# Requesting the keys' factors one pair of heads ahead, every other pair's into borrowed buffers

## The chip, the cores and the metric

One core of a Trainium2 chip runs one program. The metric is the device time of one launch in microseconds (us), as the median of several runs; the profile is of one further execution. TensorE (PE in the rows) multiplies, VectorE (DVE) and ScalarE (ACT) work elementwise, GpSimd (POOL) here only issues transfers, and so does SyncE (SP). PEld is TensorE's weight load.

## The reference

One layer of a diffusion backbone over 256 latent tokens with 256 context tokens, model width 2048: modulation from `c`, a combined input projection, attention with 8 heads beside a gated MLP over chunks, a merge with sigmoid gates, an output projection and a SwiGLU feed-forward part. What bears on the change is attention, with keys normalized by head:

```python
k = _rms(jnp.concatenate([k_nope, k_rope], axis=-1), qk_norm_k)
...
s = jnp.einsum('bqhd,bkhd->bhqk', qi, k, preferred_element_type=jnp.float32) * scale
p = jax.nn.softmax(s, axis=-1)
o = jnp.einsum('bhqk,bkhd->bqhd', p.astype(v.dtype), v, preferred_element_type=jnp.float32)
```

## The kernel before

Activations lie in the on-chip memory with channels on the 128 partitions. Weights stream through ten buffers `raw` of 128x1024 (512 KB), requested by SyncE in the program's order. Each half is split into a rounded part `whi` (ScalarE, L230) and the rest `wlo` (VectorE, L231), and the products run in both parts (`mm3`, `mm_wides`; every matmul is recorded at L244).

The layer runs in stages: modulation and input projections, the chunk MLP, queries and keys, attention, merge and output projection, feed-forward. Attention alone would leave TensorE idle while a softmax runs, so `fill(n, rate)` puts independent work between its parts: `n` halves of gate products, and for each of them `rate` steps of the second modulation (`background`; ATT_RATE is 2.9). Such a step takes one `raw` tile as it landed and adds it, scaled, into `acc` on VectorE (L416). At the end of a block of 16 tiles the sums go through DRAM: four small stores `m_d` (L439), then a load of `sh` (L442), on POOL's queue. VectorE adds a bias to `sh` at L397. These blocks are what stands on POOL's queue beside the requests of the change.

The keys are not normalized by themselves. One factor per key and head, the reciprocal root of the mean square, is computed for all heads in `rk` (to L754), stored to DRAM as `rk_d` by four stores (L757), and multiplied into the scores later. The attention loop (L776) takes the heads in four pairs. At the start of a pair two transfers (L782) request the factors of its two heads, each a row of 512 numbers repeated on 128 partitions (256 KB), into a slot of the pool `g`, which holds 60 slots of 128x512. For each of two halves `qt` of the queries the pair's scores go to two banks (L786, L790). Then for each head VectorE multiplies the scores by the factors and takes the maximum of a row (L794), makes the bias `nb` (L798), ScalarE takes the exponential with its sum `sm` (L800), VectorE inverts the sum and divides (L801, L802), and TensorE transposes the probabilities (L805) with the identity matrix in `cst`. ScalarE copies them out (L807), `fill` follows (L809), and after both halves the products with the values (L814).

`rst` (128x512) holds the reciprocal roots of the first norm; its last reader is the first modulation (L371), before the input projections end. `cst` holds constants: the identity and a permutation, then from column 2P on 512 columns of cosines and sines for the rotary step (`rcos`, `rsin`, read last at L472 and L473 for the queries), then small selection matrices. A scheduler of the framework sets the order in which each engine's queue holds its instructions, by its own estimate of when operands are ready, places slots, and adds a wait where two instructions touch the same bytes. Each engine works through its queue in that order and waits at the first instruction whose operands are missing.

Of the kernel before, what the change touches and what calls it, by code (L numbers as in the profile page):

```python
# [13 lines left out]
P = 128  # L14
# [4 lines left out]
TOK = SEQ + CTX  # L19
GRID_W = 64  # L20
HEADS = 8
# [91 lines left out]
def block_kernel(  # L113
# [25 lines left out]
    nc = tc.nc  # L139
# [13 lines left out]
    def uid():  # L153
        cnt[0] += 1
        return cnt[0]

    def slot(dt=F32):
        return gp.tile([P, 512], dt, tag="g", name=f"g{uid()}")

    def small(cols, name, bufs=8):  # L160
        return sp.tile([P, cols], F32, tag=name, name=f"{name}{uid()}", bufs=bufs)

    def mmbank():
        return pm.tile([P, 512], F32, tag="mm", name=f"mm{uid()}")

    def auxbank():
        return pa.tile([P, 512], F32, tag="aux", name=f"ax{uid()}")
# [4 lines left out]
    cst = cp.tile([P, CST_END], F32, name="cst")  # L172
# [70 lines left out]
    def mm(out, lhsT, rhs, start=True, stop=True):  # L243
        nc.tensor.matmul(out, lhsT, rhs, start=start, stop=stop)  # L244
# [33 lines left out]
    def split_to(dst_hi, dst_lo, src):  # L278
        S.activation(dst_hi, src, AF.Copy)  # L279
        V.tensor_tensor(out=dst_lo, in0=src, in1=dst_hi.bitcast(F32), op=ALU.subtract)  # L280
# [22 lines left out]
    rst = cp.tile([P, TOK], F32, name="rst")  # L303
# [150 lines left out]
    def background(rate):  # L454
        bg_state[0] += rate
        while bg_state[0] >= 1.0:
            bg_state[0] -= 1.0
            if next(bg, 1) is None:
                bg_state[1] += 1
# [166 lines left out]
    def fill(n, rate):  # L626
        for _ in range(n):
            if next(gi, 1) is None:
                background(rate)
# [59 lines left out]
    for c in range(3):  # L689
        w = W(flat(wuq, c * P * WCOLS, WCOLS), WCOLS)  # L690
        for i in range(2):
# [12 lines left out]
            else:  # L704
                S.activation(d, ps, AF.Copy, scale=pcol(PR_GQ + 1))
                r = slot()
# [48 lines left out]
    rk_d = dp.tile([HEADS, TOK], F32, name="rk_d")  # L755
    for i in range(4):
        nc.gpsimd.dma_start(rk_d[2 * i:2 * i + 2, :], rk[32 * i:32 * i + 2, :])  # L757

    fill(UQ_GATES[4], GATE_RATE)
    vals = []  # L760
    w = W(flat(wuv, 0, WCOLS), WCOLS)
# [13 lines left out]
    ao = []  # L775
    for p in range(HEADS // 2):  # L776
        pair = (2 * p, 2 * p + 1)
        rkb, pts = {}, {}
        for h in pair:
            rkb[h] = slot()  # L780
            r = 2 * (h % 4) + h // 4
            nc.gpsimd.dma_start(rkb[h], rk_d[r:r + 1, :].to_broadcast([P, 512]))  # L782
        for qt in range(2):
            ps = [auxbank(), auxbank()]
            for e, h in enumerate(pair):
                mm(ps[e], qnope[p][:, e * 256 + qt * P:e * 256 + (qt + 1) * P], kn[h], True, False)  # L786

            for e in range(2):
                rows64 = slice(e * ROPE, (e + 1) * ROPE)
                mm(ps[e], qrot[p][rows64, qt * P:(qt + 1) * P], krot[rows64, :], False, True)  # L790
            for e, h in enumerate(pair):
                t = slot()
                mx = small(1, "mx")
                V.tensor_tensor_reduce(out=t, in0=ps[e], in1=rkb[h], scale=1.0, scalar=-3.0e38,  # L794
                                       op0=ALU.mult, op1=ALU.max, accum_out=mx)
                col = qt * 8 + e * 4 + p
                nb = small(1, "nb")
                V.tensor_tensor(out=nb, in0=mx, in1=nrq[:, col:col + 1], op=ALU.mult)  # L798
                sm = small(1, "sm")
                exp = S.activation(t, t, AF.Exp, bias=nb, scale=rq[:, col:col + 1], accum_out=sm)  # L800
                V.reciprocal(sm, sm)  # L801
                V.tensor_scalar_mul(t, t, sm)  # L802
                tp = auxbank()
                for k in range(4):
                    nc.tensor.transpose(tp[:, k * P:(k + 1) * P], t[:, k * P:(k + 1) * P], ident)  # L805
                pt = slot()
                S.activation(pt, tp, AF.Copy)  # L807
                pts[h, qt] = pt
            fill(ATT_GATES[2 * p + qt], ATT_RATE)  # L809
        for h in pair:  # L810
            ops = auxbank()
            for qt in range(2):
                for k in range(4):
                    mm(ops[:, qt * P:(qt + 1) * P], vals[k * 2 + h // 4][:, (h % 4) * P:(h % 4 + 1) * P],  # L814
                       pts[h, qt][:, k * P:(k + 1) * P], k == 0, k == 3)
            t = slot(F32R)
            split_to(t[:, 0:256], t[:, 256:512], ops[:, 0:256])
            ao.append(t)
# [128 lines left out]
    for f in range(FT):  # L947
# [10 lines left out]
        pair = [mmbank(), mmbank()]  # L958
# [177 lines left out]
```

## Time and profile before

| | us |
|---|---|
| median of 3 runs (lowest to highest) | 1457.03 (1454.49 to 1457.60) |
| the profiled execution's own time | 1455.91 |
| its span, first to last instruction | 1454.1 |
| TensorE busy in it | 1422.4 (98%) |
| VectorE busy | 1018.6 (70%) |
| ScalarE busy | 772.6 (53%) |

Where the rows speak of idle time, the arrow names what ended it, inferred from the semaphores. The granted clock is TensorE's, as a share of 2.4 GHz. A landing is counted from the issue of a request to its last byte.

### The profile page before, as it was taken

The numbers are of one execution on the slowest core, as the hardware profiler recorded it, in microseconds if no ns is written. First come the engines' busy times: TensorE is split into PE (matmuls) and PEld (weight loads), VectorE is DVE, ScalarE is ACT, GpSimd is POOL, SyncE is SP. The second block draws the span as 40 slices with busy tenths as digits, with TensorE's granted clock in tenths as the row PEclk, the third lists the DMA queues.
The fourth block names the chain that finished last, engine by engine and source line by source line (L and its number), as shares of the span: only waits on it lengthen the run. The fifth ranks groups of instructions, "written<-read, shape, count | busy, mean of one in ns | idle before, by whom it ended". The sixth has DMA issues, their size and how long they took to land.

```text
span 1454.1 us, 23911 instructions
## 1 busy us (share of the span) xinstructions
PE 1422.4 (98%) x8782; PEld 1215.1 (84%) x8782; DVE 1018.6 (70%) x1738; ACT 772.6 (53%) x1432; POOL 22.2 (2%) x44
## 2 busy tenths in 40 slices
PE   6999999999989999999999999999999999999998
PEld 4898899886767799988788888888888888888887
DVE  2676579896688688999866666666666667786553
ACT  4655457555534554555566555555555554444442
POOL 0000000000101000000000000000000000000000
PEclk9999999999999999999999999999999999999999
DMA  9987874785499498999553555555555568898560
GB/s 366 350 318 266 316 297 140 253 287 190 144 313 314 175 362 329 324 353 391 175 183 135 192 188 186 192 188 189 187 190 189 188 202 308 309 361 302 198 213 33
DMA packets 104167, 356.08 MB, mean 245 GB/s; under 512 B 12520, under 2 KB 14824, under 8 KB 104048
## 3 DMA queue, kind: packets, MB, share of 16 engines
q1 hardware_dynamic: 102096, 350.82, 67.0%
q0 software_dynamic: 1952, 3.72, 1.0%
q8 instruction: 69, 1.13, 0.3%
q14 instruction: 50, 0.41, 0.1%
HBM read 352.36 MB, written 2.13 MB: 244 GB/s over the span
## 4 chain that ended last, share of the span: by engine, by line
PE 65%; DVE 4%; DMA 1%; issue 1%; ACT 0%; DVEq 0%; ACTq 0%
PE mm L244 62%; PE ax L244 2%; DVE acc L416 1%; DMA raw<-in_wmod_dram 1%; DVE wlo L231 1%; PE ax L805 0%; DVE g L802 0%; ACT g L800 0%; DVE g L405 0%; DVE g L890 0%; DVE g L794 0%; DVE g L870 0%; DVE g L892 0%; ACT whi L230 0%; DVE g L402 0%
## 5 line engine op out<-in xcount | busy, mean ns | idle before, releaser
L244 PE MATMUL mm<-g,whi 128*128 128x512 f32 (+1 forms) x3456 | 878.6, 347 | 0.8 <-ACT g L702 0.5
L230 ACT ACTIVATE whi<-raw 128x512 fp32r<-128x512 f32 x897 | 557.3, 630 | 500.9 <-PE mm L244 349.9
L231 DVE TENSOR_TENSOR wlo<-raw,whi 128x512 fp32r<-128x512 f32 x897 | 604.1, 687 | 259.1 <-ACT whi L230 253.4
L244 PE MATMUL mm<-g,wlo 128*128 128x256 f32 x2656 | 588.7, 282 | 0.6 <-DVE wlo L231 0.6
L244 PEld LDWEIGHTS mm<-g,wlo 128*128 128x128 f32 x2656 | 495.3, 190 | 79.5 <-DVE wlo L231 1.3
L244 PEld LDWEIGHTS mm<-g,whi 128*128 128x128 f32 x3456 | 540.0, 191 | 22.1 <-issue 11.0
L244 PE MATMUL mm<-whi,g 128*128 128x512 f32 x992 | 308.3, 391 | 0.0
L244 PEld LDWEIGHTS mm<-whi,g 128*128 128x128 f32 x992 | 186.2, 188 | 41.3 <-issue 2.5
L244 PE MATMUL mm<-wlo,g 128*128 128x512 f32 x496 | 193.2, 390 | 0.2 <-DVE wlo L231 0.2
L416 DVE SCALAR_TENSOR_TENSOR acc<-raw,silw,acc 128x1024 f32<-128x1024 f32 x120 | 153.4, 1278 | 17.7 <-DMA raw<-in_wmod_dram 17.1
L244 PEld LDWEIGHTS mm<-wlo,g 128*128 128x128 f32 x496 | 93.1, 188 | 21.2 <-issue 1.1
L554 DVE TENSOR_TENSOR g<-mm,g 128x512 f32<-128x512 f32 x60 | 41.1, 686 | 26.4 <-PE mm L244 25.9
L279 ACT ACTIVATE g<-g 128x256 fp32r<-128x256 f32 (+1 forms) x106 | 41.9, 414 | 13.7 <-DVE g L973 8.2
L280 DVE TENSOR_TENSOR g<-g,g 128x256 fp32r<-128x256 f32 (+1 forms) x106 | 43.2, 424 | 7.4 <-ACT g L279 7.3
L971 DVE TENSOR_TENSOR g<-mm,g 128x256 f32<-128x256 f32 x88 | 33.3, 419 | 17.3 <-ACT g L970 17.2
L970 ACT ACTIVATE g<-mm 128x256 f32<-128x256 f32 x88 | 29.0, 381 | 30.9 <-PE mm L244 30.9
L244 PE MATMUL ax<-g,g 128*128 128x128 f32 (+2 forms) x224 | 42.6, 374 | 0.0
L244 PE MATMUL ax<-raw,silw 128*32 128x256 f32 (+1 forms) x576 | 33.4, 359 | 3.7 <-DMA raw<-in_wmod_dram 3.7
L244 PEld LDWEIGHTS ax<-g,g 128*128 128x128 f32 (+1 forms) x224 | 26.6, 190 | 11.5 <-issue 9.6
L244 PEld LDWEIGHTS ax<-raw,silw 128*32 128x32 f32 x576 | 16.9, 109 | 16.0 <-DMA raw<-in_wmod_dram 5.8
L800 ACT ACTIVATE g<-g,nb,rq 128x512 f32<-128x512 f32 x16 | 13.0, 812 | 17.5 <-DVE nb L798 17.4
L375 ACT ACTIVATE g<-g,m 128x256 f32<-128x256 f32 x32 | 17.6, 592 | 8.3 <-DVE m L364 5.3
(140 smaller groups left out, 471.1 us busy)
## 6 DMA issues: line engine op xcount, KB each, us to landing
raw<-in_wmod_dram SPq DMA_DIRECT2D x192, 512.0 KB, 6.3
raw<-in_wffi_dram SPq DMA_DIRECT2D x176, 512.0 KB, 3.2
raw<-in_wffo_dram SPq DMA_DIRECT2D x88, 512.0 KB, 4.9
raw<-in_wgate_dram SPq DMA_DIRECT2D x56, 512.0 KB, 4.7
raw<-in_win_dram SPq DMA_DIRECT2D x48, 512.0 KB, 7.7
raw<-in_wout_dram SPq DMA_DIRECT2D x32, 512.0 KB, 7.5
raw<-in_wbrs_dram SPq DMA_DIRECT2D x16, 512.0 KB, 9.2
raw<-in_wbra_dram SPq DMA_DIRECT2D x16, 512.0 KB, 6.5
```

The source lines that it names most:

```text
L230: S.activation(hi[:, :e], raw[:, q:q + e], AF.Copy)
L231: V.tensor_tensor(out=lo[:, :e], in0=raw[:, q:q + e], in1=hi[:, :e].bitcast(F32), op=ALU.subtract)
L244: nc.tensor.matmul(out, lhsT, rhs, start=start, stop=stop)
L279: S.activation(dst_hi, src, AF.Copy)
L280: V.tensor_tensor(out=dst_lo, in0=src, in1=dst_hi.bitcast(F32), op=ALU.subtract)
L375: S.activation(v, v, AF.Identity, bias=m[:, 2 * jj + s:2 * jj + s + 1], scale=m[:, 2 * n + 2 * jj + s:2 * n + 1 + 2 * jj + s])
L416: V.scalar_tensor_tensor(out=acc, in0=w.raw[0], scalar=sil[:, k, 0:1], in1=acc, op0=ALU.mult, op1=ALU.add)
L554: V.tensor_tensor(out=acc[i], in0=ps, in1=acc[i], op=ALU.add)
L800: exp = S.activation(t, t, AF.Exp, bias=nb, scale=rq[:, col:col + 1], accum_out=sm)
L970: S.activation(d, ps[:, 256:512], AF.Copy)
L971: V.tensor_tensor(out=d, in0=ps[:, 0:256], in1=d, op=ALU.add)
```

## The change

The two requests move out of the loop into `key_rows(p)`. It is called for pair 0 right after the stores of `rk_d`, ahead of the gate products and the values, and for pair p + 1 at the start of pair p. Pairs 0 and 2 take slots of `g` as before; pairs 1 and 3 take `rst` and the 512 columns of cosines and sines in `cst`.

```diff
@@ -756,6 +756,17 @@
     for i in range(4):
         nc.gpsimd.dma_start(rk_d[2 * i:2 * i + 2, :], rk[32 * i:32 * i + 2, :])
 
+    rkb = {}
+
+    def key_rows(p):
+
+
+        for h in (2 * p, 2 * p + 1):
+            rkb[h] = slot() if p % 2 == 0 else (rst, cst[:, 2 * P:2 * P + TOK])[h % 2]
+            r = 2 * (h % 4) + h // 4
+            nc.gpsimd.dma_start(rkb[h], rk_d[r:r + 1, :].to_broadcast([P, 512]))
+
+    key_rows(0)
     fill(UQ_GATES[4], GATE_RATE)
...
@@ -775,11 +786,9 @@
     ao = []
     for p in range(HEADS // 2):
         pair = (2 * p, 2 * p + 1)
-        rkb, pts = {}, {}
-        for h in pair:
-            rkb[h] = slot()
-            r = 2 * (h % 4) + h // 4
-            nc.gpsimd.dma_start(rkb[h], rk_d[r:r + 1, :].to_broadcast([P, 512]))
+        pts = {}
+        if p + 1 < HEADS // 2:
+            key_rows(p + 1)
         for qt in range(2):
```

The diff also moves the scheduler's order. Lines from L757 on stand 9 to 11 lines later in the new file (L782 is now L767, L794 is L803, L802 is L811, L805 is L814).

POOL's queue from the stores of `rk_d` on, with what each request waits for (DMASW and DMAHW: a landing of POOL's or SyncE's transfers; the rest: an instruction of that engine). Before:

```order
L757 DMA rk_d<-g_4439 2x512 [waits DVE_49]
L782 DMA g_4546<-rk_d 128x512 [waits DMASW2_49,DMASW1_49,DMASW3_49,DMASW0_49,PE_49]
L782 DMA g_4548<-rk_d 128x512 [waits PE_49]
L442 DMA sh_158<-m_d_4823 128x8x1 [waits DMASW6_49,DMASW7_49,DMASW1_49,DMASW0_49]
L782 DMA g_4922<-rk_d 128x512 [waits DMAHW2_49,PE_49]
L782 DMA g_4924<-rk_d 128x512 [waits DMASW4_49,PE_49]
L439 DMA m_d_5268<-g_5266 16x1x16 [waits DMASW5_49,Activation_49]
L782 DMA g_5298<-rk_d 128x512 [waits DMAHW1_49,PE_49]
L782 DMA g_5300<-rk_d 128x512 [waits DMASW2_49,DVE_49,PE_49]
L782 DMA g_5659<-rk_d 128x512 [waits DMASW4_49,DVE_49,PE_49]
```

Now:

```order
L757 DMA rk_d<-g_4439 2x512 [waits DVE_49]
L767 DMA g_4454<-rk_d 128x512 [waits DMAHW2_49,DMASW0_49,PE_49]
L767 DMA g_4456<-rk_d 128x512 [waits DMASW1_49,PE_49]
L767 DMA rst<-rk_d 128x512 [waits DMASW2_49]
L767 DMA cst<-rk_d 128x512 [waits DMASW3_49]
L442 DMA sh_158<-m_d_4825 128x8x1 [waits DMASW3_49,DMASW2_49,DMASW4_49,DMASW1_49,DMASW0_49]
L767 DMA g_4924<-rk_d 128x512 [waits DMASW5_49,PE_49]
L767 DMA g_4926<-rk_d 128x512 [waits DMASW6_49,PE_49]
L767 DMA rst<-rk_d 128x512 [waits DMASW7_49,DVE_49]
L767 DMA cst<-rk_d 128x512 [waits DVE_49]
L439 DMA m_d_5270<-g_5268 16x1x16 [waits Activation_49]
```

Pair 1's two requests stand behind pair 0's, ahead of the first block's load of `sh`; pair 2's have its old place; pair 3's stand right behind, with a wait for VectorE.

TensorE's queue at the first transposes of pair 0 (`ax`), among the gate products (`whi` and `wlo` are the halves of a weight tile). Before:

```order
L244 MATMUL mm_4589<-g_1570,wlo_4655 128x256
L244 MATMUL mm_4590<-g_1574,wlo_4655 128x256
L244 MATMUL mm_4590<-g_1855,whi_4658 128x512
L244 MATMUL mm_4589<-g_1855,wlo_4659 128x256
L805 MATMUL ax_4565<-cst,g_4556 128x128 x4
L244 MATMUL mm_4590<-g_1855,wlo_4659 128x256
```

Now:

```order
L244 MATMUL mm_4591<-g_1273,whi_4609 128x512
L244 MATMUL mm_4592<-g_1273,whi_4609 128x512
L244 MATMUL mm_4591<-g_1273,wlo_4610 128x256
L244 MATMUL mm_4592<-g_1273,wlo_4610 128x256
L814 MATMUL ax_4567<-cst,g_4558 128x128 x4
L244 MATMUL mm_4591<-g_1277,whi_4609 128x512
L244 MATMUL mm_4592<-g_1277,whi_4609 128x512
```

The transposes have moved 15 matmuls ahead: they stood in the products of operand `g_1855`, and stand behind those of `g_1273`. On VectorE the first factor step of the pair has moved ahead of three weight splits that stood before it.

VectorE's queue at the first factor step of pair 1 (the ISA row; `rst` is the borrowed buffer). Before:

```order
L231 TENSOR_TENSOR wlo_5041<-raw_5038,whi_5040 128x512
L231 TENSOR_TENSOR wlo_5045<-raw_5038,whi_5044 128x512
L794 ISA g_4932,mx_4933<-ax_4926,g_4922 128x512
L416 SCALAR_TENSOR_TENSOR acc_4829<-raw_5084,silw,acc_4829 128x1024
L397 TENSOR_TENSOR sh_158<-sh_158,prm 128x8
L416 SCALAR_TENSOR_TENSOR acc_4829<-raw_5088,silw,acc_4829 128x1024
L801 RECIPROCAL sm_4937<-sm_4937 128x1
L231 TENSOR_TENSOR wlo_5138<-raw_5135,whi_5137 128x512
L802 TENSOR_SCALAR g_4932<-g_4932,sm_4937 128x512
```

Now:

```order
L231 TENSOR_TENSOR wlo_5043<-raw_5040,whi_5042 128x512
L803 ISA g_4934,mx_4935<-ax_4928,rst 128x512
L231 TENSOR_TENSOR wlo_5047<-raw_5040,whi_5046 128x512
L416 SCALAR_TENSOR_TENSOR acc_4831<-raw_5086,silw,acc_4831 128x1024
L810 RECIPROCAL sm_4939<-sm_4939 128x1
L397 TENSOR_TENSOR sh_158<-sh_158,prm 128x8
L416 SCALAR_TENSOR_TENSOR acc_4831<-raw_5090,silw,acc_4831 128x1024
L811 TENSOR_SCALAR g_4934<-g_4934,sm_4939 128x512
```

The factor step has moved ahead of one weight split. Between it and the division stand one split, two accumulations and the bias of `sh`, as before, in another order.

## Rows read from the trace of the kernel before

**Rows 1.** Busy us by stage: PE, PEld, DVE, ACT, POOL (instructions), clock, DMA share, GB/s
```profile
360.00:512.00 152.00, 142.15 (x780) 108.31 (x779) 112.93 (x202) 78.48 (x155) 15.04 (x27) 0.98 0.69 235
480.00:512.00 32.00, 30.10 (x184) 22.61 (x183) 17.75 (x40) 20.20 (x43) 2.27 (x5) 1.00 0.42 152
512.00:690.00 178.00, 178.00 (x1166) 161.96 (x1166) 165.19 (x242) 92.23 (x167) 6.92 (x14) 1.00 0.95 354
720.00:1440.00 720.00, 720.00 (x3813) 616.69 (x3812) 461.80 (x758) 386.12 (x706) 0.00 (x0) 1.00 0.60 210
```

**Rows 2.** TensorE's waits, 366 to 512 us: total, times, longest
```profile
PE ax L805 <- DVE g L802: 9.6, 10, 3.7
```

**Rows 3.** POOL's timeline: start, us, engine, line, operation, tiles, idle time before
```profile
366.83 2.22 POOL L757 DMA_DIRECT2D rk_d<-g  x4 [366.39 <-DVE g L294]
371.42 1.12 POOL L782 DMA_DIRECT2D g<-rk_d  x2 [2.37 <-PE mm L244]
...
404.53 1.09 POOL L782 DMA_DIRECT2D g<-rk_d  x2
...
446.76 1.09 POOL L782 DMA_DIRECT2D g<-rk_d  x2
```

**Rows 4.** Issues at 366.8, 371.4, 372.0, 404.5 and 446.8: KB, us to landing
```profile
rk_d<-g POOLq DMA_DIRECT2D x1, 4.0 KB, 3.5
...
g<-rk_d POOLq DMA_DIRECT2D x1, 256.0 KB, 3.5
...
g<-rk_d POOLq DMA_DIRECT2D x1, 256.0 KB, 4.3
...
g<-rk_d POOLq DMA_DIRECT2D x1, 256.0 KB, 7.9
...
g<-rk_d POOLq DMA_DIRECT2D x1, 256.0 KB, 6.5
```

**Rows 5.** VectorE's timeline in pairs 1 and 2
```profile
412.52 0.69 DVE L794 CUSTOM_DVE_ANT_0 g<-ax,g 128x512 f32<-128x512 f32 x1 [3.29 <-DMA g<-rk_d]
...
416.34 0.48 DVE L802 TENSOR_SCALAR g<-g,sm 128x512 f32<-128x512 f32 x1
...
422.53 0.48 DVE L802 TENSOR_SCALAR g<-g,sm 128x512 f32<-128x512 f32 x1
...
453.44 0.69 DVE L794 CUSTOM_DVE_ANT_0 g<-ax,g 128x512 f32<-128x512 f32 x1 [2.37 <-PE mm L244]
...
457.78 0.48 DVE L802 TENSOR_SCALAR g<-g,sm 128x512 f32<-128x512 f32 x1
```

**Rows 6.** TensorE's timeline in pairs 1 and 2
```profile
402.18 6.51 PE L244 MATMUL ax<-g,g 128*128 128x128 f32 x40
...
416.97 1.09 PE L805 MATMUL ax<-cst,g 128*128 128x128 f32 x4 [3.66 <-DVE g L802]
...
424.93 0.60 PE L805 MATMUL ax<-cst,g 128*128 128x128 f32 x4
...
458.41 0.63 PE L805 MATMUL ax<-cst,g 128*128 128x128 f32 x4 [2.49 <-DVE g L802]
```

**Rows 7.** Busy time in stretches of 2 us behind the two gaps
```profile
420.00:422.00 2.00, 2.00 (x7) 1.71 (x7) 1.50 (x4) 1.23 (x3) 0.00 (x0) 0.50 0.82 244
422.00:424.00 2.00, 2.00 (x12) 1.71 (x12) 2.00 (x3) 0.64 (x1) 0.00 (x0) 0.85 0.96 375
...
458.00:460.00 2.00, 1.59 (x11) 1.53 (x12) 2.00 (x4) 0.60 (x1) 0.00 (x0) 1.00 0.97 320
```

**Rows 8.** TensorE's and VectorE's timeline in pair 0
```profile
377.19 0.63 PE L244 MATMUL mm<-g,whi 128*128 128x512 f32 x2
...
380.23 0.63 PE L805 MATMUL ax<-cst,g 128*128 128x128 f32 x4 [0.21 <-DVE g L802]
...
381.20 0.69 DVE L794 CUSTOM_DVE_ANT_0 g<-ax,g 128x512 f32<-128x512 f32 x1
...
384.14 0.49 DVE L802 TENSOR_SCALAR g<-g,sm 128x512 f32<-128x512 f32 x1
```

## The prediction

> **What bounds the kernel now.** I read the table by stage first, then the waits of the attention stage, then the queues around them. The stage table shows TensorE busy for all of 512 to 690 us and of 720 to 1440 us, and for 142.15 of 152.00 us between 360 and 512, the stretch that holds attention [rows 1]. So what attention loses stays lost to the end, and what it gets back is got back, unless a later transfer takes it (a rival below). TensorE's waits between 366 and 512 us are of one kind: ten times, for 9.6 us together, the transposes of the probabilities wait for VectorE's last step, the division L802 [rows 2].
>
> Two of the ten make up 6.2 us, and both begin at the first score-times-factor step of a pair (L794). POOL's timeline shows when the keys' factors are requested: pair 1's at 404.53, pair 2's at 446.76 us, each at the start of its pair [rows 3]. The landings are 7.9 and 6.5 us after the request [rows 4], at 412.4 and 453.3. VectorE's timeline has L794 at 412.52 after 3.29 us of idleness, and at 453.44 after 2.37 [rows 5]: about 0.1 us behind the landing, both times. The second idle time is put down to TensorE; by those times it is the factors too. On TensorE each becomes a gap ahead of the transposes: 3.66 us up to 416.97 and 2.49 us up to 458.41 [rows 6]. After the longer gap the granted clock reads 0.50 (1.2 GHz); 422 to 424 has 0.85, so full speed is back at 422.6. After the shorter it stayed at 1.00 [rows 7]. Pair 3's factors are not waited for. Pair 0's come in just as VectorE turns to them: requested at 371.42 [rows 3], landed after 3.5 us [rows 4].
>
> **Pair 1.** Its factors are now requested at about 372 us and go into the two borrowed buffers, whose own readers are long done: nothing on POOL waits for them but the landing of two writes. So L794 waits for the scores alone. They are finished when the 40 matmuls of 402.18 are, at 408.69 [rows 6]. VectorE, one weight split further along, was free at 409.23 (412.52 less 3.29), so with L794 ahead of that split it is free at 408.6. I put L794 at 408.7. From L794 to the end of L802 it was 4.30 us (412.52 to 416.82 [rows 5]); the same kinds of steps stand between them in the new order. L802 then ends at 413.0, and TensorE comes to the transposes at 413.31 (416.97 less 3.66). The gap of 3.66 goes whole: **-3.7 us**, at least the 3.3 of VectorE's idleness.
>
> **The clock.** Without the gap no fall: from 416.97 to 422.6 TensorE worked at half speed, so 2.8 us are lost there. Not all of it comes back, because VectorE is next: the second head's transposes stood at 424.93 [rows 6], 7.96 us after the first, so at full speed 5.2 us after them, at 418.5. VectorE's part of that head starts 3.8 us sooner, not 6.5: L802 ran 422.53 to 423.01 there [rows 5], so 419.2 now, and the transposes follow at 419.4. I leave 0.9 us: **-1.9 us**, between -1.0 (the 0.9 twice) and -2.8.
>
> **Pair 2.** Its slots are read out by pair 0's products, so POOL requests it where pair 1's request stood, some 40 us before it is needed. L794 moves up by its idleness, L802 (ended 458.26 [rows 5]) to 455.9, and TensorE is there at 455.92 (458.41 less 2.49 [rows 6]). **-2.3 us**, between -2.1 (0.2 from L802 to the transposes) and -2.5, the whole gap.
>
> **Pair 3.** Its two requests wait on POOL for pair 1's last L794. Behind them stands the mod2 block's own store, which comes later by the program. Nothing gained, nothing lost: 0.
>
> **Pair 0.** Here the change costs something. The requests now wait for one write of the factors each, no longer for all four; the first write landed 3.5 us [rows 4] after 366.83, at 370.3, which lets the request out 0.5 us sooner, near 370.9. With 3.5 us to land and 0.1 to start, L794 comes at 374.5 instead of 375.05. But the order of TensorE's queue now has the first transposes 15 matmuls sooner: they stood at 380.23, after 0.21 us of waiting, and are now due at 377.19 [rows 8]. The second head's chain from L794 to the end of L802 took 3.43 us (381.20 to 384.63 [rows 8]); so L802 ends at 377.9, the transposes start at 378.1, and TensorE waits 0.9 where it waited 0.2: **+0.7 us**, between 0 and, if the row lands no sooner than before, +1.2. The weight splits set back behind L794 are for tiles that TensorE comes to only after the transposes' old place, over 3 us on: no cost. No instruction is added or dropped; there are eight requests before and after.
>
> Sum against the profiled execution of 1455.91 us: -3.7 -1.9 -2.3 +0.7 = -7.2, **1448.7 us**. That execution lies 1.1 us below the median shown; from the median the same gain would give 1449.8.
>
> What a request takes to land decides all this: the rows have 3.5 us in a quiet stretch, 7.9 and 6.5 in busy ones [rows 4], and my sum goes by them. The Trainium skill, "DMA: Bandwidth & Descriptors", section "Anatomy of one DMA", gives a fixed part of about 2.0 us and the bytes at 436 GB/s, by my estimate 2.6 us for 256 KB. By that, pair 1's factors would have been there at 407.1, ahead of the scores, and asking sooner would gain nothing there. The trace shows three times as long, and the measurement decides; what the rule would make of the time is the last rival.
>
> **Rivals.**
> *Pair 0 pays.* If the first row lands only when its second did (372.0 and 4.3, so 376.3 [rows 4]), since four now queue up, L794 is at 376.4, L802 ends at 379.9, and TensorE waits 2.8 us instead of 0.2. That lies between the gap that kept the clock (2.49) and the one that lost it (3.66): 1450.6, or with another 2.8 us of clock 1453.4. For it: four requests instead of two. Against: the first one issued is the first to be served in every pair of the rows.
>
> *VectorE keeps the time.* It is busy for 112.93 of the stage's 152 us [rows 1], and most of its steps take what a transfer brings; what is freed may be met at once by the next weight's landing. Then only VectorE's idleness in one pair is gained, 3.3 us: 1452.6. Against: in pair 1 the weights for the next accumulations were there by the time the factors were, since VectorE ran from L794 to L802 in 4.30 us of nearly unbroken work [rows 5].
>
> *Slower.* TensorE enters 512 to 690 some 7 us sooner, where the DMA share is 0.95 [rows 1]. Were the loads bound by the transfer engines from before 480 on, their landing would stand still, TensorE would give the gain back in one wait, and fall to half speed after it: 1455.9 +2.8 = 1458.7. The point that decides is whether the queue runs dry in between. It does: 0.42 between 480 and 512 [rows 1], where the requests wait for buffers that compute frees, so they move with it.
>
> *No effect.* L794 in pairs 1 and 2 waited for something that came together with the factors, as the row at 453.44 says in naming TensorE [rows 5], or the transfer into `cst` waits for the transposes, which read another part of that tile. Then every gap stays: 1455.9. Against: the landing is 0.1 us ahead of L794 in both pairs, and POOL's waits, printed below the diff, name no instruction of TensorE for `rst` and `cst`. The page's 2.6 us would put the landing elsewhere and so speak for this case.
>
> **How the numbers follow.** My forecast 0.74, pair 0 pays 0.12, VectorE keeps 0.06, slower 0.04, no effect 0.04. The forecast's own range, from the ends of the terms: -3.7 -2.8 -2.5 +0 = -9.0 and -3.3 -1.0 -2.1 +1.2 = -5.2, so 1446.9 to 1450.7. The runs shown lie 1.4 below to 1.7 above the profiled one; with that, and with the next two cases, 1445.5 to 1453.4. What a measurement of this kernel can tell from no change is 0.2%, 2.9 us. Faster by more: the forecast, nearly all of the next two, 0.89. Within: 0.07, no effect and what is left of those. Slower: 0.04.
>
> **What would show it.** TensorE's waits in the stage fall from 9.6 to about 5 us, with none over 1.5; the clock reads 1.00 through 410 to 430; L794 of pairs 1 and 2 starts behind the scores; pair 0's transposes have the largest wait left. Wrong if L794 is named as waiting for the factors in pair 1 or 2, if the clock falls near 380, or if the part after 512 grows.

## The result, and the profile after

The change takes 1448.37 us (median of 4 runs, 1448.01 to 1449.26) beside 1457.30 us of the kernel before on the same chip (4 runs, 1454.49 to 1457.60): the ratio is 0.9944, 95% interval 0.9927 to 0.9961. That is faster: the nearer end of the interval is 0.39% from no change, more than the 0.2% that the prediction took as the least to be told. Its profiled execution took 1448.01 us, with a span of 1446.2 and a mean granted clock of 0.997; the execution profiled before took 1455.91, 1454.1 and 0.995. Between these two profiles 7.9 us went.

The stage table first, over the stage and what follows it, each moved by the 8 us that the change gains (the columns are those of [rows 1]):

```profile
360.00:504.00 144.00, 139.60 (x782) 106.26 (x781) 112.57 (x203) 78.88 (x155) 15.15 (x28) 1.00 0.70 249
472.00:504.00 32.00, 30.38 (x187) 22.86 (x186) 18.04 (x42) 20.45 (x44) 2.61 (x6) 1.00 0.37 134
504.00:682.00 178.00, 178.00 (x1167) 161.97 (x1166) 165.52 (x242) 92.48 (x167) 6.58 (x13) 1.00 0.95 352
712.00:1432.00 720.00, 720.00 (x3813) 616.69 (x3812) 461.74 (x757) 385.60 (x705) 0.00 (x0) 1.00 0.60 210
```

TensorE is busy for 139.60 of 144 us; in [rows 1] it was 142.15 of a stage 8 us longer. The stage ends 8 us sooner, and from 504 us on the same two stretches, 178 and 720 us long, are filled as before. So the gain is made in attention and nothing takes it back. The quiet stretch ahead of 504, DMA share 0.37, is still there.

The waits of TensorE in the stage, in us, times and longest, answer to [rows 2]:

```profile
PE ax L814 <- DVE g L811: 4.2, 10, 0.7
```

Ten waits are left, 4.2 us in place of 9.6, the longest of 0.7. TensorE's timeline shows where the two long ones stood ([rows 6, 8] before; start, us, operation, tiles, wait ahead of it; each row is the four transposes of one softmax piece):

```profile
377.86 0.63 PE L814 MATMUL ax<-cst,g 128*128 128x128 f32 x4 [0.60 <-DVE g L811]
...
394.82 0.63 PE L814 MATMUL ax<-cst,g 128*128 128x128 f32 x4 [0.19 <-DVE g L811]
413.44 0.63 PE L814 MATMUL ax<-cst,g 128*128 128x128 f32 x4 [0.56 <-DVE g L811]
419.48 0.60 PE L814 MATMUL ax<-cst,g 128*128 128x128 f32 x4
...
434.95 0.63 PE L814 MATMUL ax<-cst,g 128*128 128x128 f32 x4 [0.17 <-DVE g L811]
450.50 0.63 PE L814 MATMUL ax<-cst,g 128*128 128x128 f32 x4
```

Rows of the kernel before that stand against these, beside those of [rows 6] (pair 0's second and last transposes, pair 1's last):

```profile
384.78 0.63 PE L805 MATMUL ax<-cst,g 128*128 128x128 f32 x4
...
394.52 0.63 PE L805 MATMUL ax<-cst,g 128*128 128x128 f32 x4 [0.18 <-DVE g L802]
...
440.40 0.63 PE L805 MATMUL ax<-cst,g 128*128 128x128 f32 x4 [0.17 <-DVE g L802]
```

Pair 1's first transposes wait 0.56 us where they waited 3.66, pair 2's not at all where they waited 2.49. Set against the kernel before, the running difference is +0.3 at pair 0's last transposes (394.82 against 394.52), -3.5 at pair 1's first (413.44, 416.97), -5.4 at its second (419.48, 424.93), the same at its last (434.95, 440.40), and -7.9 at pair 2's first (450.50, 458.41). There it stays.

The clock after pair 1's first transposes, in windows of 2 us:

```profile
420.00:422.00 2.00, 2.00 (x13) 1.76 (x12) 2.00 (x3) 1.12 (x2) 0.00 (x0) 1.00 1.03 414
422.00:424.00 2.00, 2.00 (x6) 0.68 (x6) 2.00 (x5) 1.29 (x3) 0.00 (x0) 1.00 1.02 410
```

The third number from the right is 1.00, that is 2.4 GHz, where [rows 7] had 0.50 and 0.85.

POOL's timeline and one landing (KB, us; pair 0's first request) tell when the factors were asked for, against [rows 3, 4]:

```profile
370.74 1.13 POOL L767 DMA_DIRECT2D g<-rk_d  x2 [1.79 <-DMA rk_d<-g]
371.85 0.56 POOL L767 DMA_DIRECT2D rst<-rk_d  x1
372.38 0.56 POOL L767 DMA_DIRECT2D cst<-rk_d  x1
404.91 1.09 POOL L767 DMA_DIRECT2D g<-rk_d  x2
425.75 0.54 POOL L767 DMA_DIRECT2D rst<-rk_d  x1 [19.75 <-DVE mx L803]
```

```profile
g<-rk_d POOLq DMA_DIRECT2D x1, 256.0 KB, 3.6
```

Pair 1's two requests leave at about 372 us, pair 2's at 404.91, some 40 us ahead of use, pair 3's behind pair 1's reading of the buffers. On VectorE the factor step L803 of pair 1 reads `rst`, 408.99 where it was 412.52, and the division L811 stands behind it:

```profile
408.99 0.69 DVE L803 CUSTOM_DVE_ANT_0 g<-ax,rst 128x512 f32<-128x512 f32 x1
...
412.81 0.48 DVE L811 TENSOR_SCALAR g<-g,sm 128x512 f32<-128x512 f32 x1
...
418.75 0.48 DVE L811 TENSOR_SCALAR g<-g,sm 128x512 f32<-128x512 f32 x1
```

None of these rows has idle time ahead of it; [rows 5] had 3.29 us.

### The profile page after: what moved, and what is told of

It is laid out like the page before. It is cut to its first block, busy times and chain, and to the rows that moved or that the text cites. A ratio compares the mean times of both kernels' runs of the same rounds, so it can differ in the third digit from the quotient of the medians.

```text
span 1446.2 us, 23902 instructions
## 1 busy us (share of the span) xinstructions
PE 1420.4 (98%) x8782; PEld 1212.5 (84%) x8782; DVE 1018.6 (70%) x1738; ACT 772.9 (53%) x1432; POOL 21.9 (2%) x44
## 4 chain that ended last, share of the span: by engine, by line
PE 88%; DVE 5%; DMA 3%; issue 2%; ACT 1%; SPq 0%; DVEq 0%; ACTq 0%; POOLq 0%
PE mm L244 82%; PE ax L244 6%; DMA raw<-in_wmod_dram 2%; DVE acc L416 1%; DVE wlo L231 1%; PE ax L814 1%; DVE g L811 0%; DMA cst<-in_cst_dram 0%; ACT whi L230 0%; PE ax L348 0%; DMA g<-rk_d 0%; DVE g L803 0%; SPq L187 0%; DVE g L291 0%; ACT g L809 0%
## 5 line engine op out<-in xcount | busy, mean ns | idle before, releaser
L231 DVE TENSOR_TENSOR wlo<-raw,whi 128x512 fp32r<-128x512 f32 x897 | 604.7, 688 | 259.6 <-ACT whi L230 252.8
L416 DVE SCALAR_TENSOR_TENSOR acc<-raw,silw,acc 128x1024 f32<-128x1024 f32 x120 | 153.5, 1279 | 17.8 <-DMA raw<-in_wmod_dram 17.2
L279 ACT ACTIVATE g<-g 128x256 fp32r<-128x256 f32 (+1 forms) x106 | 41.9, 415 | 13.3 <-DVE g L982 8.1
L280 DVE TENSOR_TENSOR g<-g,g 128x256 fp32r<-128x256 f32 (+1 forms) x106 | 43.2, 425 | 7.4 <-ACT g L279 7.2
```

What stands on the lines that cost most here:

```text
L231: V.tensor_tensor(out=lo[:, :e], in0=raw[:, q:q + e], in1=hi[:, :e].bitcast(F32), op=ALU.subtract)
L416: V.scalar_tensor_tensor(out=acc, in0=w.raw[0], scalar=sil[:, k, 0:1], in1=acc, op0=ALU.mult, op1=ALU.add)
```

## The experiments

Each kernel is compared with the kernel before on its own chip. The theory to be tested: the landing of pair 1's and pair 2's factors made TensorE wait, and the half clock followed the wait. Against it stand: the new order alone did it; less traffic in the busy stretch did it; the parts do not add up.

### One pair at a time

Pair 1 alone, by these lines against the change (the call for pair 0 ahead of the loop is taken out too):

```diff
-            rkb[h] = slot() if p % 2 == 0 else (rst, cst[:, 2 * P:2 * P + TOK])[h % 2]
+            rkb[h] = slot() if p != 1 else (rst, cst[:, 2 * P:2 * P + TOK])[h % 2]
...
-    key_rows(0)
...
-        if p + 1 < HEADS // 2:
+        if p not in (1,):
+            key_rows(p)
+        if p + 1 in (1,):
             key_rows(p + 1)
```

> Only pair 1's two rows are requested early, into rst and the cosines of cst; pairs 0, 2 and 3 ask for theirs at their own start, into slots, as in the kernel before. Theory (the landing of pair 1's rows made TensorE wait 3.66 us, and the half clock from 416.97 to 422.5 was a consequence of that wait): 3.1 us of wait and 2.6 us of half clock go, 5.7 us less than the kernel before, ratio 0.9961; the granted clock is 1.00 in every 2-us window from 404 to 424, pair 2's wait of 2.49 us stays. Rival (the clock fell for another reason, the sparse stretch of the scores): 3.1 us less, ratio 0.9979, windows at half clock remain. Rival (no pair is worth much alone, the gain is less traffic in the busy stretch, spread over the 6 moved rows): a third of 7.9, 2.6 us less, ratio 0.998.

Measured: 1452.79 us beside 1456.84, ratio 0.9968, interval 0.9955 to 0.9980. TensorE's timeline:

```profile
385.78 0.63 PE L815 MATMUL ax<-cst,g 128*128 128x128 f32 x4
...
414.17 0.63 PE L815 MATMUL ax<-cst,g 128*128 128x128 f32 x4 [0.57 <-DVE g L812]
...
435.70 0.63 PE L815 MATMUL ax<-cst,g 128*128 128x128 f32 x4 [0.17 <-DVE g L812]
455.02 1.09 PE L815 MATMUL ax<-cst,g 128*128 128x128 f32 x4 [3.81 <-DVE g L812]
462.41 0.60 PE L815 MATMUL ax<-cst,g 128*128 128x128 f32 x4
```

From 385.78 to 435.70 it is 49.92 us; the kernel before took 55.62 (384.78 to 440.40). So at pair 1 5.7 us went, as the theory has it, in wait and clock. (The time alone does not decide: the interval holds the first rival's 0.9979 too.) But pair 2 then waits 3.81 us, not 2.49, and its transposes run at half speed (1.09 us for the four, against 0.63). From 435.70 to 462.41 it takes 26.71 us, 2.65 more than the 24.06 of the kernel before in its first profile (440.40 to 464.46). That is hardly a price of this edit: two further profiles of the unchanged kernel, shown below, take 26.42 and 26.41 us for the same stretch. Pair 2's row took 7.9 us to land, against 6.5 in [rows 4]:

```profile
g<-rk_d POOLq DMA_DIRECT2D x1, 256.0 KB, 7.9
```

Pair 2 alone is the same edit with 2 in place of 1.

> Only pair 2's two rows are requested early, into rst and the cosines of cst; the other pairs ask at their own start, into slots. Theory (each pair's wait is removed by itself, and the clock falls where one wait is long enough): pair 1 keeps its wait of about 3.7 us and its 5 us at half clock, pair 2's wait of 2.49 us goes, 2.5 us less than the kernel before, ratio 0.9983; the span is about 5.4 us over the change's. Pair 1 alone, of which the earlier run showed 5.7 us gained at pair 1 and about 3 given back at pair 2 (wait 3.81 in place of 2.49, and half clock behind it), and pair 2 alone then sum to less than the change. Rival (the parts simply add up): pair 2 alone gives what pair 1 alone left of the 7.9, 4 to 5.5 us less, ratio 0.9963 to 0.9972.

Measured: 1452.37 beside 1457.51, ratio 0.9968, interval 0.9957 to 0.9980. The expected 0.9983 lies outside: pair 2 by itself is worth more than its wait in the first profile, and the rival, that the parts add up, fits. Two times 0.0032 is 0.0064, beside the change's 0.0056 (0.0039 to 0.0073). Pair 1 keeps its wait, 2.99 us, and works at half speed after it:

```profile
416.40 1.09 PE L815 MATMUL ax<-cst,g 128*128 128x128 f32 x4 [2.99 <-DVE g L812]
```

Pair 0 alone keeps its early call and has every pair in slots:

```diff
-            rkb[h] = slot() if p % 2 == 0 else (rst, cst[:, 2 * P:2 * P + TOK])[h % 2]
+            rkb[h] = slot()
...
-        if p + 1 < HEADS // 2:
+        if p not in (0,):
+            key_rows(p)
+        if p + 1 in (0,):
             key_rows(p + 1)
```

> Only pair 0's two rows are requested early, into slots, as the change does; pairs 1 to 3 as in the kernel before. Theory: the waits at pairs 1 and 2 stay (about 3.7 and 2.5 us, half clock behind the first), pair 0's transposes come 15 rows earlier in TensorE's order and wait about 0.2 us more in all: the time stays, ratio 0.9995 to 1.0005. Rival (slots held longer push pair 1's or pair 2's requests back): a wait of pair 1 or 2 longer by the delay, ratio over 1.001.

Measured: 1457.54 beside 1457.51, ratio 1.0002, interval 0.9990 to 1.0014. The order that moves pair 0's transposes is worth nothing that could be measured. This profile has the clock fall behind both of the later waits, which the first profile of the kernel before had not:

```profile
417.13 1.09 PE L816 MATMUL ax<-cst,g 128*128 128x128 f32 x4 [2.93 <-DVE g L813]
...
457.60 1.09 PE L816 MATMUL ax<-cst,g 128*128 128x128 f32 x4 [2.83 <-DVE g L813]
```

### The buffer or the place in the program

Every pair calls at its own start (`()` is empty, so the first condition always holds and the second never); only the buffers are those of the change:

```diff
-    key_rows(0)
...
-        if p + 1 < HEADS // 2:
+        if p not in ():
+            key_rows(p)
+        if p + 1 in ():
             key_rows(p + 1)
```

> Every pair asks for its rows at its own start, where the kernel before has them; only the buffers differ: pairs 1 and 3 use rst and the cosines of cst, pairs 0 and 2 slots. Theory (what held the requests back was the wait for a free slot on POOL's queue, which pair 0's last products ended at 404.5; the place in the program did not matter): pair 1's requests leave about 372, its gain of 5.7 us comes in full, ratio 0.9961, and pair 2's wait of 2.49 us stays. Rival (the place in the program sets when a request leaves): pair 1's requests leave at about 404 as before and the time stays, ratio 1.000.

Measured: 1452.47 beside 1456.84, ratio 0.9969, interval 0.9960 to 0.9979, the same as with pair 1 asked for early. POOL's timeline:

```profile
371.04 0.58 POOL L767 DMA_DIRECT2D rst<-rk_d  x1 [2.12 <-DMA rk_d<-g]
...
372.15 1.09 POOL L767 DMA_DIRECT2D g<-rk_d  x2
...
440.91 1.10 POOL L767 DMA_DIRECT2D g<-rk_d  x2
```

Pair 1's requests go out at 371.04, though they stand in the loop, and even ahead of pair 0's: given a buffer that is free, the scheduler puts them there by itself. Pair 2's, in slots, leave at 440.91, and it waits 3.49 us. So for pair 1 the borrowed buffer was all; the call one pair ahead is what moves pair 2, whose slots come free with pair 0's products. Of the two things that pair 1's request stood behind at 404.53, a slot and the place behind POOL's load of `sh`, this run does not tell which held it. (The place can hold a request by itself: with two copies, below, that load came late, and pair 2's request left right behind it, at 410.13 against 404.91 in the change.)

### Pair 0 put back

```diff
-    key_rows(0)
...
         pts = {}
+        if p == 0:
+            key_rows(0)
```

> The change, with pair 0's two requests put back to the start of the loop (ahead of pair 1's). Theory (pair 0's early request brings nothing, and cost 0.13 us of running difference at its last transposes): 7.9 to 8.2 us less than the kernel before, ratio 0.9944 to 0.9946, and the first transposes of pair 0 come where the order puts them, 15 rows later than in the change. Rival (asking for pair 0 early and the order that came with it is part of the gain): under 7.5 us less, ratio over 0.9949.

Measured: 1447.85 beside 1456.84, ratio 0.9940, interval 0.9927 to 0.9952: the change's gain without pair 0's move. Its span of 1445.5 is 0.7 under the change's, but 0.6 of that is there already when POOL stores `rk_d` (366.14 against 366.73). The two versions are the same to within what can be measured. Against the borrowed buffers in place, 1452.47 on the same chip, this run moves only the call one pair ahead, and so gives pair 2's share in another way: 4.6 us.

### No transfers for pairs 1 to 3

```diff
-        if p + 1 < HEADS // 2:
-            key_rows(p + 1)
+        for h in pair:
+            rkb[h] = rkb[h % 2]
```

> The factor rows of pairs 1 to 3 are not requested at all: these pairs multiply with pair 0's two rows, so six transfers of 256 KB are left out and the output is another one. Theory (in the change these six transfers are hidden entirely): the time of the change, 7.9 us under the kernel before within 0.4, ratio 0.9943 to 0.9949, and the same waits of TensorE in the stage, about 4.2 us. Rival (the transfers still cost the weights their bandwidth): 1.5 MB less at the rate that the DMA queues move in this stage shows up as 2 us or more under the change, ratio 0.993 or less.

Measured: 1449.70 beside 1456.84, ratio 0.9953, interval 0.9939 to 0.9966; span 1445.8. Six transfers fewer bring nothing, so in the change they are hidden, and less traffic is not the cause of the gain. (The output is another one, since pairs 1 to 3 multiply with pair 0's factors.) One wait grew, from 0.56 to 1.24 us:

```profile
403.42 0.76 DVE L609 TENSOR_TENSOR g<-mm,g 128x256 f32<-128x256 f32 x2 [1.09 <-ACT g L608]
...
413.38 0.63 PE L814 MATMUL ax<-cst,g 128*128 128x128 f32 x4 [1.24 <-DVE g L811]
```

Pair 0's second transposes came 0.7 us sooner than in the change (382.00 against 382.72), pair 1's first no sooner (413.38 against 413.44). In between VectorE stood idle for 1.09 us at L609, behind a step of ScalarE (L608) that had waited 2.04 us for the landing of the stores `m_d`; in the change L609 has no idle time ahead of it. From 404 to 424 VectorE is busy for 20.00 of 20 us, for 19.70 in the change: with so little slack, what it loses before comes out at the transposes.

### One row held back

I wanted to set the length of pair 1's wait by hand. POOL copies a piece of pair 0 into `rst` a few times (2 and 6) and only then asks for the row that goes there; pair 1's other row, into `cst`, still leaves at about 373:

```diff
-        if p + 1 < HEADS // 2:
+        if p in (1, 2):
             key_rows(p + 1)
...
+        if p == 0:
+            for _ in range(2):
+                nc.gpsimd.tensor_copy(out=rst, in_=pts[1, 1])
+            key_rows(1)
         for h in pair:
             ops = auxbank()
```

> The change with pair 1's first row alone held back: POOL first copies pair 0's last softmax piece (written at about 396) twice into rst, then asks for the row. With the issue at T, the landing 7.5 to 7.9 us later and 4.6 us from a landing to the transposes (as in the kernel before, 412.39 to 416.97), TensorE waits T - 400.6 us at pair 1's first head, where that is over 0.56. Theory (the half clock is what a wait brings that is longer than some 2.5 to 3.5 us): with a wait under 2.5 us the clock stays 1.00 behind it and the span is the change's 1446.2 plus the added wait alone; with one over 3.5 us the clock falls to half for about 5 us and 2.6 us come on top. Rival (half the clock follows any wait here, or hangs on the rest of pair 1's work): the 2-us windows behind the wait go by something else than its length.

> As the run with two copies, with six copies on POOL ahead of the request, so that the row is asked for later by four of its copies and the wait at pair 1 is longer by as much. Theory: beyond a wait of 3.5 us, the half clock follows it and costs 2.6 us besides the wait; the span is 1446.2 plus the added wait plus 2.6. If the wait is under 2.5 us, only the wait is added. Rival (the clock does not hang on the length of the wait): all windows behind it stay at 1.00, or the half-clock stretch grows with the wait.

Measured, one run each: 1453.02 us with a wait of 3.83 at pair 1 for two copies, 1451.90 with a wait of 2.17 for six. Both misses: the wait was not T - 400.6 (T was 398.86 and 405.46), and more copies made it shorter. The row had landed in both (at 406.4 and 410.8 us) before VectorE came to it (411.20 and 411.68). With two copies it was another transfer that came late, by the chain of waits (start, us, what):

```profile
400.87 7.68 DMA m_d<-g
...
409.21 6.17 DMA sh<-m_d
```

The row's request had got in front of the four small stores of `m_d` on POOL's queue. They took 7.2 to 7.8 us to land, 3.3 to 4.4 in the change, so the load of `sh` behind them came late, and its bias step on VectorE, which stands ahead of L811, had 1.56 us of idle time before it. The same stores had cost VectorE another 1.66 us, at L280: that step stood behind one of ScalarE (L279) that waited 3.24 us for their landing. With six copies, from 397.20 to 405.16, it was VectorE itself that was slow:

```profile
397.85 0.69 DVE L231 TENSOR_TENSOR wlo<-raw,whi 128x512 fp32r<-128x512 f32 x1 [1.52 <-ACT whi L230]
...
402.05 1.62 DVE L416 SCALAR_TENSOR_TENSOR acc<-raw,silw,acc 128x1024 f32<-128x1024 f32 x1
403.60 1.09 DVE L231 TENSOR_TENSOR wlo<-raw,whi 128x512 fp32r<-128x512 f32 x1
...
406.83 1.27 DVE L416 SCALAR_TENSOR_TENSOR acc<-raw,silw,acc 128x1024 f32<-128x1024 f32 x1
...
411.07 0.68 DVE L231 TENSOR_TENSOR wlo<-raw,whi 128x512 fp32r<-128x512 f32 x1
```

L803 stood 15.80 us behind pair 0's last transposes, 14.17 in the change, and the 1.6 us between them are what the wait grew by (2.17 against 0.56). What the two do tell: the clock fell behind a wait of 2.17 us, though it had stayed up behind 2.49 in [rows 7]. So the theory's threshold does not hold, and the length of a wait is not what decides by itself.

### The same programs once more

That led to a question on the first profile: is what it shows of pairs 1 and 2 the program's, or that execution's? Both kernels were profiled again, unchanged.

> The kernel before, unchanged, profiled once more. In the kernels in which pair 1 or pair 2 still waits, the stretch at half clock behind the wait was 3.4 us or 6.8 us long or absent, and did not follow the length of the wait (2.49 us: none; 2.17 us: 3.4; 2.99 us: 6.8; 3.81 us: 3.4). Theory (whether and how long the clock falls behind a wait differs between executions of the same program): this execution shows another pattern than the first (6.8 us behind pair 1, none behind pair 2), with pair 1's and pair 2's waits within 1 us of 3.7 and 2.5. Rival (the pattern belongs to the program): 6.8 us behind pair 1 and none behind pair 2 again.

> The kernel before, unchanged, profiled a third time. Theory: over the three profiles of this program the half-clock stretches behind pairs 1 and 2 differ, and at least one of them shows half clock behind pair 2, as the profile with pair 0 alone moved did. Rival: all three are the same, 6.8 us behind pair 1 and none behind pair 2.

> The change, unchanged, profiled once more. Theory: with no wait over 0.7 us in the stage there is nothing for the clock to fall behind: 1.00 throughout from 400 to 470, waits of TensorE on its transposes 4 to 5 us in all. Rival (the clock falls here by itself in some executions): a stretch at half clock without a wait of over 1 us ahead of it.

The second profile of the kernel before (1459.15 us), and the third (1456.89 us):

```profile
417.95 1.09 PE L805 MATMUL ax<-cst,g 128*128 128x128 f32 x4 [3.76 <-DVE g L802]
426.07 0.60 PE L805 MATMUL ax<-cst,g 128*128 128x128 f32 x4
...
460.35 0.63 PE L805 MATMUL ax<-cst,g 128*128 128x128 f32 x4 [3.28 <-DVE g L802]
467.97 0.60 PE L805 MATMUL ax<-cst,g 128*128 128x128 f32 x4
```

```profile
416.77 1.09 PE L805 MATMUL ax<-cst,g 128*128 128x128 f32 x4 [3.29 <-DVE g L802]
423.58 0.60 PE L805 MATMUL ax<-cst,g 128*128 128x128 f32 x4
...
458.08 1.09 PE L805 MATMUL ax<-cst,g 128*128 128x128 f32 x4 [3.53 <-DVE g L802]
465.45 0.60 PE L805 MATMUL ax<-cst,g 128*128 128x128 f32 x4
```

The half clock in the third profile, behind each of its two waits:

```profile
416.00:418.00 2.00, 1.23 (x5) 1.25 (x6) 1.92 (x4) 0.38 (x2) 0.00 (x0) 0.63 0.88 305
418.00:420.00 2.00, 2.00 (x8) 1.73 (x7) 1.86 (x5) 0.89 (x2) 0.00 (x0) 0.52 0.90 285
...
456.00:458.00 2.00, 0.00 (x0) 0.00 (x0) 2.00 (x5) 1.58 (x4) 0.00 (x0) 0.87 0.94 328
458.00:460.00 2.00, 1.92 (x8) 1.85 (x9) 2.00 (x3) 0.60 (x1) 0.00 (x0) 0.50 0.93 315
460.00:462.00 2.00, 2.00 (x11) 1.73 (x10) 1.09 (x5) 0.50 (x1) 0.00 (x0) 0.78 1.03 397
```

A window's time at half clock is twice what its clock lacks of 1.00, times its 2 us: (0.37 + 0.48) x 4 = 3.4 us at pair 1 and (0.13 + 0.50 + 0.22) x 4 = 3.4 at pair 2, where the fall begins 0.5 us before the wait is over. The three profiles of one program so have 6.8 and 0, 6.8 and 3.4, 3.4 and 3.4 us at half clock behind pairs 1 and 2. The theory is borne out. In both new profiles the first factor step of pair 2 is named as waiting for the factors (3.16 and 3.41 us), where [rows 5] named TensorE. The change again has none, its waits are 4.1 us in all, and it took 1447.73 us.

All profiles in one table. Waits are TensorE's on its transposes in the stage; the time at half clock is summed as above, in finer windows. The last column is the span less the waits and less half the time at half clock. Where the clock fell before the wait was over (1.2 us before in the first profile, at most 1.5, with the borrowed buffers in place), half of that stretch is taken off twice, so the column is too small there by up to 0.7:

| kernel | waits | at half clock | span | rest |
|---|---|---|---|---|
| before, three profiles | 9.6, 10.5, 10.3 | 6.8, 10.3, 6.8 | 1454.1, 1457.4, 1455.1 | 1441.1, 1441.8, 1441.4 |
| pair 0 alone | 9.5 | 6.8 | 1454.3 | 1441.4 |
| pair 1 alone | 7.9 | 3.4 | 1451.7 | 1442.1 |
| borrowed buffers in place | 7.2 | 6.8 | 1451.3 | 1440.7 |
| pair 2 alone | 6.2 | 6.8 | 1451.2 | 1441.6 |
| row held back, 2 and 6 copies | 7.3, 6.0 | 3.4, 3.4 | 1451.3, 1450.1 | 1442.3, 1442.4 |
| the change, two profiles | 4.2, 4.1 | 0, 0 | 1446.2, 1446.0 | 1442.0, 1441.9 |
| pair 0 put back | 3.8 | 0 | 1445.5 | 1441.7 |
| no transfers for pairs 1 to 3 | 5.2 | 0 | 1445.8 | 1440.6 |

The spans differ by 12 us, the rest by under 2. The waits and the half clock account for what these kernels differ in, to within about 1 us either way.

## Why the prediction was right, and where its sum was not

The forecast of 1448.7 us stands beside 1448.37, and its case is the one that came: the landings, not the order or the traffic, held the two pairs up. By its own steps, profile against profile:

**Pair 1's wait, -3.7.** The first transposes moved by 3.8 us against pair 0's last. L803 came at 408.99, foreseen 408.7; L811 ended at 413.3, foreseen 413.0. But only 3.1 us of this is wait (3.66 to 0.56), less than the term's own least of 3.3. The other 0.7 is order: the scheduler put pair 1's first transposes ahead of four products that stood before them. TensorE's timeline has 14 products with the high and 14 with the low halves between the first and the second transposes before, 16 and 16 now, and such a group of four takes 0.70 us.

**The clock, -1.9.** From the first to the second transposes it took 7.96 us, and takes 6.04: -1.9. This is the term whose reason failed. "Not all of it comes back, because VectorE is next" is not what the trace shows: the second transposes at 419.48 have no wait, L811 having ended at 419.2. All of the clock came back, 7.96 less (6.04 less 0.70), 2.6 us, inside the bounds; the 0.7 that is missing is the four products from above. The two errors cancel in the sum of both terms, -5.7 against -5.6. That VectorE is close behind was right all the same: it is what the first transposes still wait 0.56 us for, and at the second it had ended 0.25 us before.

**Pair 2, -2.3.** 2.5 us went in this pair of profiles (15.55 us from pair 1's last transposes to pair 2's first, 18.01 before), the whole gap. As the worth of the change at pair 2 the term is too small, because the profile it was read from was the mildest of three at this place: the waits were 2.49, 3.28 and 3.53 us, and in the other two half clock followed. By the three profiles pair 2 cost on the mean 3.1 us of wait, and from its first to its second transposes 6.05, 7.62 and 7.37 us, so 1.0 of clock. Pair 1 cost 3.0 of wait beyond the 0.56 that stays (3.57 on the mean), and 2.3 of clock (7.96, 8.12 and 6.81 us against 5.34).

**Pair 3, 0, and pair 0, +0.7.** Pair 3 neither gained nor lost: from pair 2's first transposes on the difference stays -7.9. Pair 0's four transposes took 0.4 us more, counted from the store of `rk_d` (28.09 us to the last of them, 27.69 before). The row landed after 3.6 us and L803 came at 374.54, as foreseen; the wait was 0.60, not 0.9. Alone it is not to be measured.

**The sum.** -7.2 was forecast against the profiled execution, and -7.9 came (-0.1 ahead of the stage, +0.4, -3.8, -1.9, -2.5). Between the medians it is -8.9, and the mean terms of the three profiles give it: -5.3 - 4.1 + 0.4 = -9.0. So that 1448.7 and 1448.37 lie 0.3 us apart is in part luck: the sum was 1.7 short of the gain between the medians, and it was taken off an execution 1.4 us below the median of the kernel before (1455.91, 1457.30). The prediction's other reckoning, the same gain from the median, 1449.8, shows the shortfall: 1.4. The three profiles of the kernel before differ by the very waits and clock that the change removes; that all its executions do (1453.78 to 1461.04 over 18 runs on one chip, 1456.02 to 1458.44 over 13 on another) is not shown. The change's own 4 runs lie within 1.3 us, but the version with pair 0 put back, which has none of these waits in its profile either, ran from 1447.02 to 1450.47.

**The rivals.** *No effect* fell with the first profile, and with it the estimate of 2.6 us for a 256 KB row from the Trainium skill, "DMA: Bandwidth & Descriptors", section "Anatomy of one DMA": the row asked for first landed after 3.4 to 4.2 us in the quiet stretch at 371, and rows asked for first in the busy ones after 5.3 to 8.0. *Pair 0 pays* did not come, since the first row issued was the first to land; its price leaned on a clock that falls only past 2.49 us, and the wait of 2.17 showed that to be no bound. *VectorE keeps the time* is true of the 0.56 us that are left at pair 1's first transposes. *Slower*, the gain taken back by the loads after 504, is excluded by the window of 178.00 busy us. One of the signs named did not come: the largest wait left is not pair 0's (0.64) but one at pair 3 (0.74).

No version of these beats the change measurably. What is left to win in the stage is ten short waits, 4.2 us in all, behind VectorE's steps; nothing was tried on them.

## What to carry to other kernels

A wait of the matrix engine for a late transfer cost its length here and, in most cases, some time at half speed, so a term for it needs two parts and a spread; one profile shows one draw of both. Ask for small broadcast rows before the busy stretch, and where the scheduler holds them back, look for a buffer whose readers are done: that alone moved pair 1's request here. Before a small difference between two kernels' profiles is put down to the edit, profile one of them again: of the 2.65 us that pair 2 seemed to lose with pair 1 alone, 0.3 were left beside the later profiles of the unchanged kernel.

## What had not been expected of the hardware

The granted clock fell to half at waits of 2.17, 2.83, 2.93, 2.99, 3.28, 3.29, 3.49, 3.53, 3.66, 3.76, 3.81 and 3.83 us and not behind one of 2.49, and each time it was down for 3.4 or 6.8 us, without following the length of the wait (3.81: 3.4; 2.99: 6.8). The fall came between 1.5 us before the end of the wait (3.49) and 1.4 us after it (2.17). The three profiles of the unchanged kernel differ in this. The Trainium skill, "TensorE: Matmul & The Clock Gate", section "Part 1: The HAM clock gate", says of a kernel's start that the gate's timing runs free of the kernel, so that the same kernel meets it differently from run to run. The three profiles agree, with waits in the middle of a kernel. What of the time around a wait decides, beside its length, was not tried and stays open.

Between the first and the last of POOL's six copies, two of VectorE's three weight splits L231 took 1.09 us in place of 0.68 (the first took 0.69), the three accumulations L416 1.51 to 1.62 in place of 1.27, and the one scaling L414 1.10 in place of 0.75; the copies themselves took 0.61 to 1.50. The Trainium skill, "SBUF — State Buffer", section "Who interferes with whom", says that a VectorE instruction with two inputs in SBUF contends with a POOL instruction that reads SBUF; the rows agree in that both kinds with two inputs, L231 and L416, were slowed and were back to 0.68 and 1.27 when the copies had ended. L414 has one input in SBUF and was slowed too. One of the two slow splits, at 401.03, lies mostly beside POOL's stores and not its copies, by the profile's rough spans for POOL; this stays open.

A 256 KB row asked for just ahead of 1 KB stores on POOL's queue went with landings of 7.2 to 7.8 us for these stores, 3.3 to 4.4 in the change, and 3.9 to 4.2 with six copies, where the stores went first. Here the order on a queue mattered even though each of these transfers is small; it is one run with the row ahead.
